# A hybrid decoder layer on one core: fill between chained steps kept on account, the output gate's projection in other loops, states loaded earlier, single-row matmuls in bursts of two tiles

## The chip, the core and the metric

The kernel runs on one core of a Trainium2 chip. Its engines run side by side and wait for each other through semaphores: TensorE (PE for its matmuls, PEld for its weight loads), VectorE (DVE), ScalarE (ACT), GpSimd (POOL) and SyncE (SP), which here issues most DMAs. The metric is device time in microseconds (us); lower is better.

## What is computed

One layer of a decoder serves a prompt of 512 rows and a group of samples, 8 x 4 = 32 rows, with the same weights, all in float32, width 1024. Cut to what matters:

```
h = rms_norm(x, g_mix_pre);  z = h @ w_in
q, k, v, o, gates = mLSTM columns of z (4 heads x 128);  dq, dk, dv = attention columns
h_ml = rms_norm(mlstm(q, k, v, gates, state)) * sigmoid(o)
a = (softmax(dq1 dk1) - lam * softmax(dq2 dk2)) dv        # samples: over cached pages too
x = x + rms_norm(concat(h_ml, rms_norm(a)) @ w_out)
x = x + rms_norm(cross_attention(x, memory))
c = causal_conv3(rms_norm(x) @ w_up);  x = x + rms_norm((silu(c_g) * c_a) @ w_down)
```

The mLSTM of the prompt runs in chunks with a carried matrix state (a chain); that of the samples reads and updates a 128 x 128 state for each of 8 samples and 4 heads. New states, keys, values and conv rows are outputs as well.

## The kernel before

Weights are cast into a high and a low float32r half (`split`, lines 140 to 143), and each product of a k tile is three matmuls. `gemmA` puts token rows out on partitions (blocks 0 to 3 of 128 prompt rows, block 4 with the 32 sample rows); `gemmB` puts weight columns out on partitions, for results that are wanted transposed. Weights pass through staging tiles `wst` (six) into `wslot` tiles (four), in the order of a plan (`Weights`). The 32 sample rows, the "single rows" of the change's title, do not use the split: `sample_mm` (line 359) multiplies them in plain float32 with the staged weights, a pair of k tiles as four matmuls of 32 columns, each to its own 32 partitions of PSUM. In the profile such a matmul is two records, so a pair is x8; in the order it is x4.

The program's text is handed to a scheduler that orders each engine's instructions itself; the text sets priorities and dependences.

Much of the middle is chained work in small steps: the chunks of the prompt's mLSTM (`ml_own`, `ml_state`, `ml_rows`, four steps), the state updates of the samples (`mls_update`, eight, two groups of four samples by four heads), the loop over cached keys (`dk_load`, `dk_turn`, `dk_scores`) and over cached values (`dv_load`, `dv_out`), both with the prompt's attention (`da_soft`, `da_turn`, `da_av`, `da_end`) between their steps. Large matmuls are dealt out between these steps by `Fill`: a queue of generators (`gemmA` for `dk`, `dq`, `dv`, then `gemmB` for the output gate `soT`), each of whose pieces tells its length in us (2.99 for a k tile of all five blocks, 1.36 for two k tiles of `gemmB`); `F.run(amount)` takes pieces until the amount is used up. A last piece that goes beyond the amount is not counted against the next call.

A state update (lines 943 to 959): the states of a group, `Cs`, are loaded (tag `T2`, eight buffers for all small tiles), the queries are multiplied with all four heads' states of a group (`mlsi`, line 949), the update is a matmul `mlus` (line 952), four VectorE steps change `Cs` in place (line 954), and it is written out (line 956); group 1's loads are issued behind group 0's outputs. The gate's sigmoid and the transposition of the mLSTM's result stand in `out_gate`, added to the fill in the loop over cached keys. PSUM has five tiles `mm` and three tiles `at`, the latter for `mlsi`, `mlus`, and the transpositions `tpk` of cached keys.

Of the kernel before, what the change touches and what calls it, by code (L numbers as in the profile page):

```python
# [15 lines left out]
P = 128  # L16
# [6 lines left out]
H = 4  # L23
# [50 lines left out]
def kernel(ctx: ExitStack, tc: tile.TileContext, I, O):  # L74
# [60 lines left out]
    dma = nc.sync.dma_start  # L135
# [191 lines left out]
    allb = [0, 1, 2, 3, 4]  # L327

    class Fill:


        def __init__(self):
            self.q = []

# [3 lines left out]
        def run(self, amount=1e9):  # L338
            while amount > 0 and self.q:
                try:  # L340
                    amount -= next(self.q[0])
                except StopIteration:
                    self.q.pop(0)

    F = Fill()
# [28 lines left out]
    def gemmA(xt, nk, blocks, evac, block_major=False, before=None, mid=None, late=False):  # L374
# [15 lines left out]
        if block_major:  # L390
            slots = [W.get() for _ in range((nk + 1) // 2)]
            for b in blocks:
                if before:
                    before(b)
                ps[b] = mmp()
                for k in range(nk):
                    if k == MIDK and mid:
                        mid()
                    one(b, k, slots[k // 2])
                    if b == blocks[-1] and k % 2 == 1:  # L400
                        W.free()
                evac(b, ps[b])
                yield 5.1
        else:
            for b in blocks:
                ps[b] = mmp()
            behind = []
            for k in range(nk):
                if k % 2 == 0:
                    s = W.get()  # L410
                    if 4 in blocks:
                        behind.append((k, s))
                        if not late:
                            one(4, *behind.pop(0))
                for b in blocks:
                    if b < 4:
                        one(b, k, s)
                if k % 2 == 1:
                    if len(behind) > 1:
                        one(4, *behind.pop(0))  # L420
                    if not late or k > 1:
                        W.free()
                yield sum(0.64 if b < 4 else 0.43 for b in blocks)
            for k, s in behind:
                one(4, k, s)
                W.free()
            for b in blocks:
                evac(b, ps[b])
            yield 0
# [336 lines left out]
    def ev_dv(b, ps):  # L766
# [4 lines left out]
        else:  # L771
# [3 lines left out]
    soT = S([P, H, ROWS], F32, "soT")  # L775
    F.add(gemmA(hT, 8, allb, ev_dk), gemmA(hT, 8, allb, ev_dq), gemmA(hT, 8, allb, ev_dv),
          gemmB(hT, [ev_T(soT, h) for h in range(H)]))

# [39 lines left out]
    def ml_own(b):  # L818
        c0 = b * P
        dms[b] = ml_scores(b)  # L820
        pk = at("mlk")
        for h in range(H):
            tr(pk[:, h * P:(h + 1) * P], kT[:, h, c0:c0 + P], ident)
        wks[b] = T2([P, H, P], "wk")
        VTT(out=wks[b], in0=v2(pk, P), in1=gt4[:, b, 3].unsqueeze(2).broadcast_to([P, H, P]), op=MUL)
        F.run(6)

    def ml_state(b):
# [6 lines left out]
        for hp in range(2):  # L835
# [9 lines left out]
            else:  # L845
                VCP(out=Cn[:, 2 * hp:2 * hp + 2], in_=v2(pu[:, :258], 129))
        F.run(3)

    def ml_rows(b):
# [20 lines left out]
        ml_norm(b, num[:, :, 0:P], num[:, :, P], mlh[b])  # L870
        F.run(3)

# [10 lines left out]


    sm_t = ml_scores(4)
    pk = at("mlks")
# [42 lines left out]
    pi = at("mlsi")  # L929
    csts, vzs = {}, {}  # L930

    def mls_values(i):
# [4 lines left out]
            in1=con("selX")[:, 4 * g:4 * g + 4].unsqueeze(2).broadcast_to([P, 4, P]), op=MUL)  # L937

    def mls_load(g, h):
        csts[g, h] = T2([P, 4, P], "Cs")  # L940
        dma(out=csts[g, h], in_=I["state_ml_C"][0, 4 * g:4 * g + 4, h].rearrange("b d e -> d b e"))

    def mls_update(i):
# [13 lines left out]
        if g == 0:  # L957
            mls_load(1, h)
        F.run(2.5)

    for h in range(H):
        mls_load(0, h)
    run(pipe(2 * H, mls_values, mls_update))
# [251 lines left out]

    W.nslots = 2
    prompt = pipe(4 * H, da_soft, lambda i: None, da_turn, da_av, da_end)
    sall = S([P, NB, 260], F32, "das")
    nm, su = small(NB, "snm"), small(NB, "ssu")
    for t, _ in enumerate(pipe(NB, dk_load, dk_turn, dk_scores)):  # L1220
        if t == 3:
            F.add(out_gate())
        F.run(2.5)
        next(prompt)
        F.run(2.5)
    aw, az = sample_softmax(sall, su, cv, con("selD"), "da")
# [23 lines left out]
    for t, _ in enumerate(pipe(NB, dv_load, lambda b: None, dv_out)):  # L1250
        if t % 2 == 0:
            next(prompt, None)
        F.run(2)
    for h in range(H):
# [364 lines left out]
    for gi, js in enumerate(groups):  # L1619
# [6 lines left out]
        nk = len(js)  # L1626

        def one(b, ps, i, s):
            n = P if js[i] < 21 else 64
            t = act[i // 2][:n, i % 2]  # L1630
            st, en = i == 0, i == nk - 1
            if b == 4:
                if i % 2 == 0:
                    sample_mm(ps, [acs[i], acs[i + 1]], s[1], st, i == nk - 2)
                return
# [34 lines left out]
        if not last:  # L1670
            for n0 in (0, 512):
                ps = {b: mmp() for b in allb}
                for i in range(nk):
                    if i % 2 == 0:
                        s = W.get()
                    for b in sorted(allb, reverse=i % 2 == 0):
                        one(b, ps[b], i, s)
                    if i % 2 == 1 or i == nk - 1:
# [6 lines left out]
        def chunk(b, n0):  # L1685
            while len(wd) < (nk // 2 if n0 == 0 else nk):
                wd.append(W.get())
            ps = mmp()
            for i in range(nk):
                one(b, ps, i, wd[(n0 and nk // 2) + i // 2])  # L1690
# [104 lines left out]
```

## Time and profile before

| what | us |
|---|---|
| median of 3 runs (1000.03 to 1001.18) | 1000.25 |
| the profiled execution's own time | 1001.39 |
| its span, first to last instruction | 999.6 |
| TensorE, sum of matmuls of `sample_mm` (line 366): hidden rows x256, FFN x176 | 20.4, 13.8 |
| `gemmB` (line 452) with `fT`, 1872 matmuls | 235.7 |
| the three matmuls of the down projection (lines 1638 to 1640) | 70.7, 69.5, 69.0 |

Times in the profile are from one execution, whose own time is in the table. A row of the chain of waits gives start, length, and what it was; a row of stages gives each engine's busy time in a stretch; a group gives its busy time, the mean of one in ns, and the idle time of its engine before it.

### The profile page before, as it was taken

What the parts mean: (1) busy time and instruction counts of PE and PEld (TensorE: products, weight loads), DVE (VectorE), ACT (ScalarE), POOL (GpSimd) and SP (SyncE); (2) the same over time, 40 slices, a digit from 0 to 9 for tenths busy, and PEclk for the clock granted to TensorE, in tenths of its full rate; (3) what the DMA queues carried; (4) which work ended last, traced back from release to release, by engine and by line L of the source; (5) the groups of instructions that cost most, each with busy time, mean ns of one, the idle gap of its engine ahead of it and who ended that gap; (6) DMA issues with size and microseconds to landing.
All of it is one profiled execution on the core that took longest, in us unless ns stands there. A gap on an engine that the chain in (4) does not pass through costs nothing.

```text
span 999.6 us, 17060 instructions
## 1 busy us (share of the span) xinstructions
PE 970.7 (97%) x6615; PEld 811.2 (81%) x6615; DVE 599.6 (60%) x1129; ACT 389.3 (39%) x746; POOL 196.1 (20%) x389
## 2 busy tenths in 40 slices
PE   8999999999799999999999999999999999999994
PEld 5899777889555778998767789989987997997983
DVE  5835324643586457643653578827848685775677
ACT  5654313434376447633552444242212222222232
POOL 6610000112332114500000264301101110010115
PEclk9999999999799999999999999999999999999997
DMA  8950234151634167785851673143143214215013
GB/s 278 296 162 14 72 85 130 43 183 55 176 109 136 61 210 233 250 260 166 277 214 43 195 237 107 43 129 91 41 115 87 84 46 127 90 42 145 25 47 110
DMA packets 120401, 130.26 MB, mean 130 GB/s; under 512 B 8423, under 2 KB 85832, under 8 KB 120320
## 3 DMA queue, kind: packets, MB, share of 16 engines
q1 hardware_dynamic: 114136, 125.69, 41.0%
q10 hardware_dynamic: 6184, 3.48, 1.2%
q8 instruction: 52, 0.85, 0.4%
q14 instruction: 29, 0.24, 0.1%
HBM read 112.22 MB, written 16.93 MB: 129 GB/s over the span
## 4 chain that ended last, share of the span: by engine, by line
PE 84%; DMA 5%; DVE 5%; issue 2%; POOL 1%; ACT 1%; SPq 0%; DVEq 0%; POOLq 0%; ACTq 0%
PE mm L452 31%; PE mm L386 6%; PE mm L387 6%; PE mm L388 6%; PE mm L440 5%; PE mm L1638 4%; PE mm L1640 4%; PE mm L1639 4%; PE mm L366 3%; PE sda L1179 2%; PE tpk L1384 2%; PE cpo L1365 1%; PE sca L1335 1%; PE ssc L1394 1%; PE oda L1205 1%
## 5 line engine op out<-in xcount | busy, mean ns | idle before, releaser
L142 ACT CAST wslot<-wst 128x1024 fp32r<-128x1024 f32 (+1 forms) x127 | 131.1, 1036 | 280.2 <-issue 81.5
L452 PE MATMUL mm<-fT,wslot 128*128 128x256 f32 (+1 forms) x1872 | 235.7, 288 | 0.0
L452 PEld LDWEIGHTS mm<-fT,wslot 128*128 128x128 f32 x1872 | 234.7, 188 | 0.7 <-issue 0.4
L143 DVE TENSOR_TENSOR wslot<-wst,wslot 128x1024 fp32r<-128x1024 f32 (+1 forms) x127 | 155.0, 1223 | 107.0 <-ACT wslot L142 106.9
L1638 PE MATMUL mm<-wslot,act 128*128 128x512 f32 (+1 forms) x176 | 70.7, 409 | 0.0
L1639 PE MATMUL mm<-wslot,act 128*128 128x512 f32 (+1 forms) x176 | 69.5, 395 | 0.0
L1640 PE MATMUL mm<-wslot,act 128*128 128x512 f32 (+1 forms) x176 | 69.0, 397 | 0.0
L1545 POOL COPY cvo<-u 128x2 f32<-128x2 f32 x43 | 16.2, 377 | 222.9 <-DVE u L1543 222.9
L386 PE MATMUL mm<-wslot,hT 128*128 128x512 f32 x128 | 51.9, 408 | 0.0
L452 PE MATMUL mm<-hT,wslot 128*128 128x288 f32 (+1 forms) x384 | 51.4, 290 | 0.0
L387 PE MATMUL mm<-wslot,hT 128*128 128x512 f32 x128 | 51.2, 400 | 0.0
L388 PE MATMUL mm<-wslot,hT 128*128 128x512 f32 x128 | 50.7, 397 | 0.0
L452 PEld LDWEIGHTS mm<-hT,wslot 128*128 128x128 f32 x384 | 48.9, 188 | 0.9 <-issue 0.8
L1638 PEld LDWEIGHTS mm<-wslot,act 128*128 128x128 f32 (+1 forms) x176 | 33.1, 189 | 17.7 <-issue 8.6
L1540 DVE TENSOR_TENSOR u<-mm,rsb 128x256 f32<-128x256 f32 x43 | 18.1, 423 | 43.5 <-PE mm L452 43.4
L1640 PEld LDWEIGHTS mm<-wslot,act 128*128 128x128 f32 (+1 forms) x176 | 33.0, 188 | 7.5
L1639 PEld LDWEIGHTS mm<-wslot,act 128*128 128x128 f32 (+1 forms) x176 | 33.1, 188 | 6.5
L1557 ACT ACTIVATE c<-c 128x560 f32<-128x560 f32 x21 | 14.1, 672 | 56.8 <-DVE c L1551 56.7
L1551 DVE SCALAR_TENSOR_TENSOR c<-u,cvT,c 128x560 f32<-128x560 f32 x43 | 34.3, 798 | 0.8
L1550 DVE SCALAR_TENSOR_TENSOR c<-u,cvT,c 128x560 f32<-128x560 f32 x43 | 34.1, 793 | 0.1
L1651 DVE TENSOR_TENSOR yp<-mm,yp 128x512 f32<-128x512 f32 x40 | 27.3, 688 | 9.5 <-PE mm L1640 9.4
L386 PEld LDWEIGHTS mm<-wslot,hT 128*128 128x128 f32 x128 | 24.0, 188 | 10.3 <-issue 5.8
(458 smaller groups left out, 1879.5 us busy)
## 6 DMA issues: line engine op xcount, KB each, us to landing
wst<-in_w_up_dram SPq DMA_DIRECT2D x42, 512.0 KB
wst<-in_w_in_dram SPq DMA_DIRECT2D x28, 512.0 KB
wst<-in_w_down_dram SPq DMA_DIRECT2D x20, 512.0 KB
wst<-in_cache_mem_k_dram SPq DMA_DIRECT2D x16, 512.0 KB
vt<-in_cache_mem_v_dram SPq DMA_DIRECT2D x8, 1024.0 KB
wst<-in_w_mk_dram SPq DMA_DIRECT2D x8, 512.0 KB
xb<-in_x_prompt_dram SPq DMA_DIRECT2D x8, 512.0 KB
wst<-in_cache_dk_dram SPq DMA_DIRECT2D x16, 256.0 KB
```

The lines of the kernel that those rows point to most:

```text
L142: nc.scalar.copy(out=hi, in_=src)
L143: (eng or nc.vector).tensor_tensor(out=lo, in0=src, in1=f32(hi), op=SUB)
L386: mm(ps[b], lhsT=xt.hi(k, c0, c0 + n), rhs=s[:, 0, kk, :], start=(k == 0), stop=False)
L387: mm(ps[b], lhsT=xt.hi(k, c0, c0 + n), rhs=s[:, 1, kk, :], start=False, stop=False)
L388: mm(ps[b], lhsT=xt.lo(k, c0, c0 + n), rhs=s[:, 0, kk, :], start=False, stop=(k == nk - 1))
L440: mm(ps, lhsT=s[:, l, k, :], rhs=x(k, c0, c1), start=(k == 0 and j == 0), stop=(k == 7 and j == 2))
L452: mm(ps[i], lhsT=s[:, l, k, :], rhs=x(k, c0, c1), start=(k == 0 and j == 0), stop=(k == 7 and j == 2))
L1550: STT(out=c, in0=u[:, 1:EXT - 1], scalar=w[1], in1=c, op0=MUL, op1=ADD)
L1551: STT(out=c, in0=u[:, 0:EXT - 2], scalar=w[0], in1=c, op0=MUL, op1=ADD)
L1638: mm(ps, lhsT=t[:, 0, c0:c0 + P], rhs=s[:n, 0, i % 2, :], start=st, stop=False)
L1639: mm(ps, lhsT=t[:, 0, c0:c0 + P], rhs=s[:n, 1, i % 2, :], start=False, stop=False)
L1640: mm(ps, lhsT=t[:, 1, c0:c0 + P], rhs=s[:n, 0, i % 2, :], start=False, stop=en)
```

## The change

It changes five things. `Fill` keeps an account: what a call takes too much is owed, and paid by the next calls; the amounts are changed with it. The gate's projection leaves the first queue, which is emptied ahead of the loop over cached keys, and is queued there, with 0.9 (twice a step) and 1 us a step. The loads of group 0's states stand ahead of the samples' scores. `gemmA` and the down projection collect the sample rows of two k-tile pairs, and put them out as one burst. The diff, cut to what matters:

```diff
@@ -330,17 +330,21 @@
 
 
         def __init__(self):
-            self.q = []
+            self.q, self.due = [], 0
 
         def add(self, *gens):
             self.q.extend(gens)
 
         def run(self, amount=1e9):
-            while amount > 0 and self.q:
+
+            self.due += amount
+            while self.due > 0 and self.q:
                 try:
-                    amount -= next(self.q[0])
+                    self.due -= next(self.q[0])
                 except StopIteration:
                     self.q.pop(0)
+            if not self.q:
+                self.due = 0
 
     F = Fill()
 
@@ -410,19 +414,22 @@
                     s = W.get()
                     if 4 in blocks:
                         behind.append((k, s))
-                        if not late:
-                            one(4, *behind.pop(0))
+                        if k % 4 == 2 and not late:
+                            while behind:
+                                one(4, *behind.pop(0))
                 for b in blocks:
                     if b < 4:
                         one(b, k, s)
                 if k % 2 == 1:
-                    if len(behind) > 1:
-                        one(4, *behind.pop(0))
+                    if k == 5:
+                        while len(behind) > 1:
+                            one(4, *behind.pop(0))
                     if not late or k > 1:
                         W.free()
                 yield sum(0.64 if b < 4 else 0.43 for b in blocks)
             for k, s in behind:
                 one(4, k, s)
+            if behind:
                 W.free()
             for b in blocks:
                 evac(b, ps[b])
@@ -773,8 +780,7 @@
             dma(out=O["s_dv"][0].rearrange("b t h d -> (b t) (h d)"), in_=dvS)
 
     soT = S([P, H, ROWS], F32, "soT")
-    F.add(gemmA(hT, 8, allb, ev_dk), gemmA(hT, 8, allb, ev_dq), gemmA(hT, 8, allb, ev_dv),
-          gemmB(hT, [ev_T(soT, h) for h in range(H)]))
+    F.add(gemmA(hT, 8, allb, ev_dk), gemmA(hT, 8, allb, ev_dq), gemmA(hT, 8, allb, ev_dv))
 
 
     def ml_scores(b):
@@ -823,7 +829,7 @@
             tr(pk[:, h * P:(h + 1) * P], kT[:, h, c0:c0 + P], ident)
         wks[b] = T2([P, H, P], "wk")
         VTT(out=wks[b], in0=v2(pk, P), in1=gt4[:, b, 3].unsqueeze(2).broadcast_to([P, H, P]), op=MUL)
-        F.run(6)
+        F.run(5)
 
     def ml_state(b):
         if b % 2 == 0:
@@ -844,7 +850,7 @@
                         op0=MUL, op1=ADD)
             else:
                 VCP(out=Cn[:, 2 * hp:2 * hp + 2], in_=v2(pu[:, :258], 129))
-        F.run(3)
+        F.run(2.5)
 
     def ml_rows(b):
         c0 = b * P
@@ -868,7 +874,7 @@
             else:
                 VCP(out=nv, in_=v2(pn[:, :258], 129))
         ml_norm(b, num[:, :, 0:P], num[:, :, P], mlh[b])
-        F.run(3)
+        F.run(2.5)
 
     run(pipe(4, ml_own, ml_state, ml_rows))
     C = Cs[3]
@@ -882,6 +888,14 @@
     dma(out=O["p_ml_n"][0, 0], in_=nrow)
 
 
+    csts, vzs = {}, {}
+
+    def mls_load(g, h):
+        csts[g, h] = T2([P, 4, P], "Cs")
+        dma(out=csts[g, h], in_=I["state_ml_C"][0, 4 * g:4 * g + 4, h].rearrange("b d e -> d b e"))
+
+    for h in range(H):
+        mls_load(0, h)
     sm_t = ml_scores(4)
     pk = at("mlks")
     for h in range(H):
@@ -927,18 +941,12 @@
     dma(out=O["s_ml_n"][0].rearrange("b h d -> (b h) d"), in_=nrow1)
 
     pi = at("mlsi")
-    csts, vzs = {}, {}
-
     def mls_values(i):
 
         g, h = i // H, i % H
         vzs[i] = T2([P, 4, P], "vz", F32R)
         GTT(out=vzs[i], in0=f32(vS[:, h, :]).unsqueeze(1).broadcast_to([P, 4, P]),
             in1=con("selX")[:, 4 * g:4 * g + 4].unsqueeze(2).broadcast_to([P, 4, P]), op=MUL)
-
-    def mls_load(g, h):
-        csts[g, h] = T2([P, 4, P], "Cs")
-        dma(out=csts[g, h], in_=I["state_ml_C"][0, 4 * g:4 * g + 4, h].rearrange("b d e -> d b e"))
 
     def mls_update(i):
         g, h = i // H, i % H
@@ -956,10 +964,8 @@
         dma(out=O["s_ml_C"][0, 4 * g:4 * g + 4, h].rearrange("b d e -> d b e"), in_=cs_t)
         if g == 0:
             mls_load(1, h)
-        F.run(2.5)
-
-    for h in range(H):
-        mls_load(0, h)
+        F.run(3.2)
+
     run(pipe(2 * H, mls_values, mls_update))
     pn = at("mlsn")
     for h in range(H):
@@ -1214,15 +1220,17 @@
     STT(out=cv, in0=con("cB"), scalar=nlam, in1=con("cA"), op0=MUL, op1=ADD)
 
     W.nslots = 2
+    F.run()
+    F.add(gemmB(hT, [ev_T(soT, h) for h in range(H)]))
     prompt = pipe(4 * H, da_soft, lambda i: None, da_turn, da_av, da_end)
     sall = S([P, NB, 260], F32, "das")
     nm, su = small(NB, "snm"), small(NB, "ssu")
     for t, _ in enumerate(pipe(NB, dk_load, dk_turn, dk_scores)):
         if t == 3:
             F.add(out_gate())
-        F.run(2.5)
+        F.run(0.9)
         next(prompt)
-        F.run(2.5)
+        F.run(0.9)
     aw, az = sample_softmax(sall, su, cv, con("selD"), "da")
     F.run(4)
     pz = Z("pz")[:, :NS]
@@ -1250,7 +1258,7 @@
     for t, _ in enumerate(pipe(NB, dv_load, lambda b: None, dv_out)):
         if t % 2 == 0:
             next(prompt, None)
-        F.run(2)
+        F.run(1)
     for h in range(H):
         mm(ops[NS * h:NS * h + NS, :P], lhsT=anew[:, h].rearrange("p b t -> p (b t)"), rhs=dvS[:, h * P:(h + 1) * P],
            start=False, stop=True)
@@ -1625,13 +1633,19 @@
         act, acs = acts[gi], acss[gi]
         nk = len(js)
 
+        behind = []
+
         def one(b, ps, i, s):
             n = P if js[i] < 21 else 64
             t = act[i // 2][:n, i % 2]
             st, en = i == 0, i == nk - 1
             if b == 4:
-                if i % 2 == 0:
-                    sample_mm(ps, [acs[i], acs[i + 1]], s[1], st, i == nk - 2)
+
+                behind.append((i, s))
+                if i % 4 == 2 or i == nk - 2:
+                    for j, t in behind:
+                        sample_mm(ps, [acs[j], acs[j + 1]], t[1], j == 0, j == nk - 2)
+                    behind.clear()
                 return
             s = s[0]
             c0 = b * P
@@ -1674,7 +1688,8 @@
                     if i % 2 == 0:
                         s = W.get()
                     for b in sorted(allb, reverse=i % 2 == 0):
-                        one(b, ps[b], i, s)
+                        if b < 4 or i % 2 == 0:
+                            one(b, ps[b], i, s)
                     if i % 2 == 1 or i == nk - 1:
                         W.free()
                 for b in allb:
@@ -1686,7 +1701,7 @@
             while len(wd) < (nk // 2 if n0 == 0 else nk):
                 wd.append(W.get())
             ps = mmp()
-            for i in range(nk):
+            for i in range(0, nk, 2 if b == 4 else 1):
                 one(b, ps, i, wd[(n0 and nk // 2) + i // 2])
             add_y(b, ps, n0)
 
```

What the scheduler makes of it is seen in the order of instructions. TensorE at the down projection of the first FFN group (`act` the gated rows, `acs` their sample rows), before:

```order
L452 MATMUL mm<-fT_6087,wslot 128x288
L366 MATMUL mm<-wst,acs 32x256 x4
L1638 MATMUL mm<-wslot,act 128x512
L1639 MATMUL mm<-wslot,act 128x512
L1640 MATMUL mm<-wslot,act 128x512
```

and in the changed kernel, some thirty matmuls of the prompt later (its lines 370 and 1652 to 1654 are lines 366 and 1638 to 1640 of before):

```order
L1652 MATMUL mm<-wslot,act 128x512
L1653 MATMUL mm<-wslot,act 128x512
L1654 MATMUL mm<-wslot,act 128x512
L370 MATMUL mm<-wst,acs 32x256 x8
L1654 MATMUL mm<-wslot,act 128x512
```

The burst at the start of the group is gone; it stands with the second one, further down, and the two are one.

TensorE at the end of the state updates, before (`sda` and its mask `cb` belong to the prompt's attention, `mlsn` to the samples' result, `tpk` to the first cached keys):

```order
L1179 MATMUL sda<-dkT,dqT 128x128
L1180 LDWEIGHTS cb
L1180 MATMUL sda<-cb 128x128
L952 MATMUL mlus<-vz,kS 128x512
L949 MATMUL mlsi<-Cs,qzm 32x128 x14
L952 MATMUL mlus<-vz,kS 128x512 x4
L966 MATMUL mlsn<-tb,mlD 32x128 x4
L1158 MATMUL tpk<-cpk,wst 128x128 x16
```

and in the changed kernel (lines 957, 960, 972 and 1164 are 949, 952, 966 and 1158 of before; 459 is 452, the gate's projection):

```order
L960 MATMUL mlus<-vz,kS 128x512
L459 MATMUL mm<-hT_255,wslot 128x288
L459 MATMUL mm<-hT_255,wslot 128x256
L459 MATMUL mm<-hT_255,wslot 128x288
L459 MATMUL mm<-hT_256,wslot 128x256
L459 MATMUL mm<-hT_256,wslot 128x288
L957 MATMUL mlsi<-Cs,qzm 32x128 x13
L459 MATMUL mm<-hT_255,wslot 128x256
L459 MATMUL mm<-hT_255,wslot 128x288
L960 MATMUL mlus<-vz,kS 128x512 x3
L972 MATMUL mlsn<-tb,mlD 32x128 x4
L1164 MATMUL tpk<-cpk,wst 128x128 x16
```

Matmuls of the gate's first head now stand between the later updates; the last three `mlus` still follow each other.

SP's queue around the state loads, before:

```order
L882 DMA out_dram<-nrow 4x128
L900 DMA nrow_2292<-in_state_ml_n_dram 32x128
L941 DMA Cs<-in_state_ml_C_dram 128x4x128
L927 DMA out_dram<-nrow_2321 32x128
L941 DMA Cs<-in_state_ml_C_dram 128x4x128 x5
L956 DMA out_dram<-Cs 128x4x128 x2
L941 DMA Cs<-in_state_ml_C_dram 128x4x128 x2
L956 DMA out_dram<-Cs 128x4x128 x5
```

and in the changed kernel (895 and 964 are 941 and 956 of before; 777 the outputs of `dv`, 246 the gate's weights, 1051 the gathers of cached keys):

```order
L895 DMA Cs<-in_state_ml_C_dram 128x4x128
L941 DMA out_dram<-nrow_1971 32x128
L895 DMA Cs<-in_state_ml_C_dram 128x4x128
L964 DMA out_dram<-Cs 128x4x128 x2
L777 DMA out_dram<-dvN 128x512 x3
L895 DMA Cs<-in_state_ml_C_dram 128x4x128
L246 DMA wst<-in_w_in_dram 128x8x128 x2
L1051 ISA
L1051 DMA wst<-in_cache_dk_dram 128x512
```

Before, all eight loads of states stood close together, with twelve gathers of keys ahead of them. Now the fifth to seventh are shown here, and the eighth follows behind seven gathers.

## The prediction

> **What bounds the kernel now.** I read the page's busy shares first, then its slices.
>
> ```profile
> span 999.6 us, 17060 instructions
> PE 970.7 (97%) x6615; PEld 811.2 (81%) x6615; DVE 599.6 (60%) x1129; ACT 389.3 (39%) x746; POOL 196.1 (20%) x389
> PEclk9999999999799999999999999999999999999997
> ```
>
> TensorE is named busy for 970.7 of 999.6 us, so what shortens its work, or fills a hole in it, shortens the kernel, and no other engine is near. The clock row has two dips: one behind the end, and one in the eleventh slice, near 260 us. So next I asked for the stages around that dip (columns: length, then busy time of PE, PEld, DVE, ACT, POOL with counts, granted clock, DMA share, GB/s).
>
> ```profile
> 255.20:268.00 12.80, 7.33 (x48) 3.68 (x48) 8.44 (x33) 2.23 (x10) 5.14 (x5) 0.65 0.46 137
> 268.00:273.00 5.00, 5.00 (x26) 3.64 (x27) 2.65 (x9) 1.62 (x5) 0.95 (x3) 0.52 0.98 294
> 273.00:307.00 34.00, 32.57 (x229) 19.59 (x233) 27.82 (x75) 24.76 (x80) 11.34 (x13) 1.00 0.36 110
> 307.00:332.00 25.00, 24.40 (x233) 13.94 (x226) 17.52 (x34) 17.19 (x48) 4.57 (x6) 1.00 0.52 174
> ```
>
> The first row is the tail of the state updates of the samples: TensorE idle for 12.80 - 7.33 = 5.47 us. Row two is the first cached keys, at half clock. Rows three and four are the loop over cached keys and the one over cached values: idle 1.43 + 0.60 = 2.03 us. The chain of waits says why the first hole is there (start, length, what).
>
> ```profile
> 250.90 0.41 PE mlsi L949 x7
> 251.31 1.63 DVE Cs L954 x6
> ...
> 253.18 4.60 DMA out_dram<-Cs
> ...
> 257.80 2.97 DMA Cs<-in_state_ml_C_dram
> ...
> 260.81 1.92 PE mlsi L949 x26
> ...
> 264.01 1.62 DVE Cs L954 x6
> ...
> 267.86 3.65 PE tpk L1158 x16
> 271.51 1.03 PE ssc L1164 x8
> ...
> 274.08 0.88 PE tpk L1158 x8
> 274.96 0.57 PE ssc L1164 x8
> ```
>
> A state is updated, written out (4.60 us), only then is its buffer free for the next load (2.97 us), and `mlsi` waits for that load. No projection is left by then to fill the time: the gate projection has ended at 253 us.
>
> **Term 1, bursts of single rows.** A pair of k tiles costs four matmuls of 32 columns, recorded as eight. The chain around a single and a double burst:
>
> ```profile
> 649.45 0.24 PE mm L1640
> 649.68 0.57 PE mm L366 x8
> 650.25 0.43 PE mm L1638
> ...
> 658.57 0.24 PE mm L1640
> 658.80 1.00 PE mm L366 x16
> 659.80 0.43 PE mm L1638
> ```
>
> The matmul behind a burst holds the chain 0.43 us, against 0.24 for its like ahead of it, 0.19 more. A single burst so costs 0.57 + 0.19 = 0.76, a double one 1.00 + 0.19 = 1.19, and two singles made one save 2 x 0.76 - 1.19 = 0.33 us. Counted in the order on TensorE, 41 runs become 30: 11 x 0.33 = 3.6 us, of which four are in the conv FFN, one for each group of four tiles. Their other half brings nothing, since there the order of before already had x8. Over all 32-column work, changes between narrow and wide matmuls fall from 203 to 173, that is by 15 round trips; 11 are the bursts, the other four (mainly `mlsi`, which stood as 1, 1, 1, 13 and is now 16) would bring 1.3 us at the same price. Ends -3.6 and -5.0; I take **-5.0**, since a round trip is the same thing there.
>
> **Term 2, the state updates.** What is lost in the first two stages is the idle 5.47 us and the half clock. For the latter: `tpk` took 3.65 us for 16, against 2 x 0.88 at full clock, 1.9 more; `ssc` 1.03 against 0.57, 0.5 more; 26 records of `mlsi` 1.92 against 26 x 0.41 / 7 = 1.52, 0.4 more. Together 2.8, and the loss is 8.3 us. With the fill on account the dv projection reaches into the updates, and the gate projection's first head stands between the later ones, so the first wait (a load behind an output) has work beside it. Two pieces stay. One is the last four updates: they read the last four loaded states, and TensorE has little to put beside them.
>
> ```profile
> 263.49 4.23 DVE L954 SCALAR_TENSOR_TENSOR Cs<-Cs,dec,mlus 128x128 f32<-128x128 f32 x16 [3.81 <-PE mlus L952]
> PE mlsi L949 <- DMA Cs<-in_state_ml_C_dram: 3.5, 2, 1.9
> 269.83 2.56 SPq L1045 DMA_DIRECT2D wst<-in_cache_dk_dram  x4
> wst<-in_cache_dk_dram SPq DMA_DIRECT2D x16, 256.0 KB
> ```
>
> VectorE needs 4.23 us for those 16 steps, and the next `tpk` waits for a PSUM tile that they hold; beside them the new order has 13 `mlsi` (26 records, 1.5 us), two gate matmuls, three `mlus` and four `mlsn`, some 2.2 us in all: 2.0 us stay. The other is the eighth load: on SP's queue it now stands behind two weight tiles (512 KB each) and seven key gathers of 256 KB (0.64 us apiece on the queue, by 2.56 for four). These 2.8 MB need 9.6 us at the 294 GB/s of stage two. They can start when the dv projection's sample bursts let go of the staging tiles, and from there TensorE has, by the order, some 11 us until the `mlsi` that need the eighth. So nothing to 4 us; I take 1.0, near the even race. Ends: -8.3 (all goes) and +0.5 (the first piece stays whole at a half clock, and 4 us more wait for the load). Taken: -8.3 + 3.0 = **-5.3**.
>
> **Term 3, the loops over cached tokens.** Three heads of the gate projection, 144 matmuls, come here; they cost nothing in sum, having left the stretch before.
>
> ```profile
> 671.11 35.94 PE mm L452 x288
> ```
>
> At 35.94 / 288 = 0.125 us that is 18 us of work for steps that now take 34.0 / 10 = 3.4 us and hold 1.43 us of plain idle. VectorE was busy 27.82 of 34, and loses here the gate's multiplications, so TensorE becomes the longer by far, and the idle in both loops goes: -2.0. More may go, since "busy" covers waits as well (weight loads are busy 19.59 of 34 only): down to -5.0. Against it, ScalarE:
>
> ```profile
> 253.59 0.66 ACT L987 ACTIVATE soT<-soT 128x544 f32<-128x544 f32 x1
> 254.26 1.28 ACT L1183 ACT_TABLE_LOAD   x1
> 255.55 0.37 ACT L1183 ACTIVATE pda<-sda,nm 128x128 f32<-128x128 f32 x1
> L617 ACT COPY soT<-mm 128x256 f32<-128x256 f32 (+1 forms) x8 | 2.7, 388 | 16.3 <-PE mm L452 16.3
> ```
>
> The four sigmoids of the gate now stand among the softmax exponentials, so eight table loads are in the loops where the four of before were ahead of them: 8 x 1.28 + 4 x 0.66 + 2.7 = 15.6 us more on an engine that was busy 24.76 of 34. In 34 + 18 = 52 us that is 40.4, covered, unless the exponential behind a load is the one that TensorE waits for; also the gate's two accumulators leave three of five `psm` tiles to the loop. Bounds are nothing and the 17.2 us of rival (c); I take +0.8, 0.2 for each sigmoid, since the cover is there. Taken: **-1.2**. The Trainium skill ("ScalarE: Activation LUTs", What ACT_TABLE_LOAD costs) says that each switch also drains for about 1.38 us; by its price the loops would carry 51 of 52 us on ScalarE, an estimate, and the gain here would be gone. This trace does not agree: the exponential starts at 255.55, as the load ends.
>
> **Nothing for the rest.** The stretch with the chained steps, before:
>
> ```profile
> 97.00:216.00 119.00, 119.00 (x667) 89.68 (x660) 50.44 (x121) 36.44 (x68) 9.31 (x15) 1.00 0.33 91
> ```
>
> TensorE is never idle in it, and VectorE, the busiest of the chain's engines, is so 42% of the time. A step gets about 10 us of fill instead of some 21, since an overshoot is now paid back. Ten us still lie between a step's matmuls and the next step's, so I cost it at nothing; if VectorE's chain showed through at the end of each of four steps, at half a microsecond each, 2 us. A burst for two pairs holds the staging tiles two k tiles longer; the loads behind it start later, at a DMA share of 0.33, and are cost at nothing too, ends 0 and +1.
>
> **The sum.** -5.0 - 5.3 - 1.2 = -11.5 on the profiled execution's own 1001.39 us (span 999.6): 989.9. That execution was 1.14 above the median of 1000.25, so **988.8 us**. Own range of this case 985 to 993.
>
> **The rivals.**
> (a) *The cover is wider than I say*: all of term 2 goes, and term 3 reaches -5.0. For it: weight loads idle for 14 of 34 us. Against: the 16 steps on VectorE. 1000.25 - 5.0 - 8.3 - 5.0 = 982.0. Chance 0.15.
> (b) *The wait moves to the eighth load*: behind the gathers it comes 4 us late, not 1, and the tail falls to half clock again (2.8). 988.8 + 3.0 + 2.8 = 994.6. For it: SP issues in order, and the dip of before came although the longest of those waits was 1.9 us. Chance 0.18. The Trainium skill ("TensorE: Matmul & The Clock Gate", Part 1) has the clock fall after an idle window of about 3.4 us; by that the tail, whose waits are each near 1 us, would stay at full clock, and (b) would be 991.8. The rows speak against so simple a rule: clock down within 255 to 260 us with no idle of 3.4 us.
> (c) *Slower: the exponentials wait behind the sigmoids.* At each of four places TensorE stands for two loads, a sigmoid, and the restart of one softmax step: 2 x 1.28 + 0.66 = 3.2, plus the restart, taken as three times the 0.37 us of an exponential, 1.1; 4 x 4.3 = 17.2 in place of 0.8: 1005.2. It decides from 3.6 us a place on (13.5 us more than forecast). Against it: two steps lie between an exponential and its transposition, some 10 us with the fill. Chance 0.08.
> (d) *It doesn't do what it says*: the fill is spent elsewhere, terms 2 and 3 are zero, and only the eleven bursts count: 996.6. Chance 0.07.
>
> **How the numbers follow.** Forecast 0.52. The likeliest is 988.8. The range 981 to 997 takes in (a), (b) and (d) and leaves out (c) and the tails, less than 2 in 10. About 0.2%, 2 us, is what a measurement can tell from no change: faster means below 998.2, with the forecast, (a), (b) and most of (d): 0.92, less 0.05 for the tail of the forecast and of (d) that reach into no change: 0.87. Same: 0.05. Slower, above 1002.3, is (c): 0.08.
>
> **What would show it.** Double bursts (x16) in the FFN where x8 stood, the following matmul still at 0.43. In the state updates: no chain piece of an output followed by a state load; a wait of `mlsi` under 1.5 us, then some 2 us ahead of `tpk`; the clock row without its middle dip. In the key loop, gate matmuls between `ssc` and `oda`, and idle of TensorE below 1 us with more than 44 us for the ten steps. It is wrong if `sda` waits for `pda` at the sigmoids, if `mlsi` waits longer than before for a state, or if the dip is still there.

## The result, and the profile after

The changed kernel takes 1012.11 us (median of 5 runs, 1010.07 to 1013.53), the kernel before 1001.18 in the same session: ratio 1.0097, 95% interval 1.0079 to 1.0116. It is slower by about 1%; the prediction was 988.8, with a range that ended at 997. The page after, its span, busy shares and the row of the granted clock:

```profile
span 1008.3 us, 17081 instructions
...
PE 973.2 (97%) x6615; PEld 816.6 (81%) x6615; DVE 601.2 (60%) x1129; ACT 393.3 (39%) x750; POOL 196.5 (19%) x389
...
PEclk9999999989989799999999999999999999999998
```

TensorE is named busy for 2.5 us more than before although it does the same matmuls with fewer changes between narrow and wide ones, and the one dip in the middle has become three. One stretch holds the difference: from the first matmuls of `v` (97.9 us) to the last one of the projection with `w_out`. Ahead of it TensorE's idle time differs by 0.3 us; behind it the new one gains 1.7 us, 1.5 of them in the conv FFN. The row of that stretch, before and after (length, busy time of PE, PEld, DVE, ACT, POOL, clock, DMA share, GB/s):

```profile
97.90:384.90 287.00, 279.50 (x1792) 207.14 (x1789) 145.88 (x356) 124.32 (x290) 53.23 (x77) 0.98 0.38 115
```

```profile
97.90:395.30 297.40, 283.87 (x1801) 211.94 (x1800) 147.17 (x356) 128.80 (x294) 53.00 (x76) 0.95 0.35 111
```

It is 10.4 us longer. Idle of TensorE goes from 7.5 to 13.5 us (length less busy), and the clock from 0.98 to 0.95: the trace has it at half from 218.28 for 6.83 us, from 286.55 for 6.83 and from 330.92 for 13.65, together twice the 13.65 us of before. That costs at most 6.8 us more, an estimate that takes TensorE at half speed for all of it. With the 6.0 us of idle it is 2.4 us more than the 10.4, about what the bursts bring by the run of them alone below.

By stage (state updates, loop over keys, its end, loop over values up to the first projection matmul):

```profile
206.80:246.30 39.50, 34.03 (x264) 25.88 (x261) 29.57 (x93) 11.56 (x27) 9.66 (x11) 0.91 0.61 198
246.30:297.80 51.50, 48.88 (x351) 36.02 (x344) 24.60 (x74) 33.21 (x89) 9.53 (x17) 0.93 0.33 106
297.80:312.30 14.50, 14.03 (x91) 8.97 (x90) 6.21 (x16) 9.74 (x28) 2.36 (x3) 1.00 0.00 0
312.30:339.80 27.50, 22.53 (x197) 12.04 (x196) 17.64 (x31) 15.38 (x36) 9.10 (x10) 0.84 0.46 159
```

Three stages have idle and a low clock: 5.5 us idle in the updates, 2.6 in the loop over keys, 5.0 in the loop over values, where before TensorE missed 0.6. The idle of the updates is as long as before (5.5 us); that of the loop over values is new. The chain of waits says what each is. In the updates:

```profile
213.39 1.01 PE mlsi L957 x32
214.40 0.44 PE mlus L960
...
215.13 0.87 DVE Cs L962 x3
...
216.02 2.83 DMA out_dram<-Cs
...
218.94 0.23 DVE rp L739
```

A state is written out, and only then does `rp` start, the temporary of the rotation of `dq`: it is a `T2` tile, as the states are. So not only a load, but the fill itself now waits for an output. In the loop over keys:

```profile
282.08 0.66 ACT soT L993
...
284.02 1.28 ACT L1189
285.30 0.01 issue
285.31 0.57 ACT pda L1189 x2
285.89 0.04 issue
285.93 1.07 PE sda L1185 x2
```

A sigmoid, a table load (the row of ScalarE without a tile), the exponential, and then the scores `sda` that wait for it: rival (c), at this place and at 267 us, in the waits of TensorE (total, times, longest):

```profile
PE sda L1185 <- ACT pda L1189: 2.2, 2, 1.5
```

In the loop over values, where most is lost, the waits of ScalarE, and SP's queue:

```profile
ACT wslot L142 <- DMA wst<-in_w_out_dram: 4.7, 1, 4.7
```

```profile
257.61 59.26 SPq L1051 DMA_DIRECT2D wst<-in_cache_dv_dram  x14
316.98 6.67 SPq L227 DMA_DIRECT2D wst<-in_w_out_dram  x6
```

The six staging tiles are full of cached values from early on, and the transfers stand still: 0 GB/s in the row of 297.80 to 312.30. The weights of the projection can be loaded only when the first matmuls with values (`ops`) let tiles go. ScalarE's next instruction is the cast of such a tile, so that it stands for 4.7 us, and behind it the softmax of the prompt's attention (`pda` its exponentials, `aT` their transposes, `dao` its copied outputs):

```profile
PE oda L1211 <- ACT dao L1213: 1.5, 1, 1.5
PE tpa L1201 <- DVE pda L1193: 1.3, 1, 1.3
PE sda L1185 <- ACT pda L1189: 1.2, 1, 1.2
PE oda L1211 <- ACT aT L1203: 1.1, 1, 1.1
```

Four waits of TensorE, about 5 us, and the half clock that follows them.

### The profile page after: what moved, and what is told of

Read it like the earlier page. It is cut to its first block, busy times and chain, and to the rows that moved or that the text cites. A ratio compares the mean times of both kernels' runs of the same rounds, so it can differ in the third digit from the quotient of the medians.

```text
span 1008.3 us, 17081 instructions
## 1 busy us (share of the span) xinstructions
PE 973.2 (97%) x6615; PEld 816.6 (81%) x6615; DVE 601.2 (60%) x1129; ACT 393.3 (39%) x750; POOL 196.5 (19%) x389
## 4 chain that ended last, share of the span: by engine, by line
PE 79%; DMA 6%; DVE 6%; issue 3%; ACT 3%; POOL 2%; SPq 1%; DVEq 0%; POOLq 0%; ACTq 0%
PE mm L459 30%; PE mm L390 6%; PE mm L391 5%; PE mm L392 5%; PE mm L447 5%; PE mm L1652 4%; PE mm L1654 4%; PE mm L1653 4%; PE mm L370 3%; DMA xb<-x_d 2%; PE tpk L1392 1%; PE sda L1185 1%; DMA wst<-in_w_mk_dram 1%; PE cpo L1373 1%; PE sca L1343 1%
## 5 line engine op out<-in xcount | busy, mean ns | idle before, releaser
L459 PE MATMUL mm<-hT,wslot 128*128 128x256 f32 (+1 forms) x384 | 55.5, 298 | 0.0
L459 PEld LDWEIGHTS mm<-hT,wslot 128*128 128x128 f32 x384 | 51.1, 194 | 2.8 <-issue 1.9
L1665 DVE TENSOR_TENSOR yp<-mm,yp 128x512 f32<-128x512 f32 x40 | 27.3, 689 | 13.7 <-PE mm L1654 13.6
L1185 PE MATMUL sda<-dkT,dqT 64*128 64x128 f32 (+3 forms) x64 | 28.5, 527 | 3.5 <-ACT pda L1189 3.4
```

The source lines that it names most:

```text
L459: mm(ps[i], lhsT=s[:, l, k, :], rhs=x(k, c0, c1), start=(k == 0 and j == 0), stop=(k == 7 and j == 2))
L1185: mm(sv[c], lhsT=dqT[rr, h, c0:c0 + P], rhs=dkT[rr, h, 0:nk], start=True, stop=False)
```

## The experiments

Ratios are against the kernel before, run on the same chip beside them; us in brackets behind a ratio are medians. The medians of before differ a little from session to session (1000.45 to 1001.19), so where two other kernels are compared, it is by their distances from the before of their own session; the changed kernel is 10.9 us above its own. A ratio is not the quotient of two medians: by the ratios such distances come out up to some 2 us different (18.8 in place of 20.0, 3.3 in place of 5.4), so none of them is surer than that.

**The bursts alone** (the kernel before with the changes to `gemmA` and to the down projection, measured twice):

```diff
-                        if not late:
-                            one(4, *behind.pop(0))
+                        if k % 4 == 2 and not late:
+                            while behind:
+                                one(4, *behind.pop(0))
```

> The kernel before with the bursts of two k-tile pairs alone (gemmA and the down projection); fill without account, amounts, gate and state loads as before. If a round trip between narrow and wide matmuls costs 0.33 us wherever it stands, this is 3.6 to 5.0 us faster than before, about 1.3 of it in the conv FFN. Rival: the bursts hold staging tiles longer and delay the weights behind them, then it is within 1 us of before, with new waits of mm for wslot.

> The bursts alone once more, to size them: the first seven runs gave 2.4 us, their profiled execution 4.7 us less than that of before. If a round trip costs what the prediction took: ratio 0.995; if half of that: 0.9975.

Measured: 0.9975, interval 0.9964 to 0.9986 (998.04), and again 0.9964, 0.9951 to 0.9977 (997.62): 2.4 and 3.3 us faster. The eleven bursts were priced at 3.6, which lies at the edge of the first interval (1.4 to 3.6 us) and inside the second (2.3 to 4.9). The further 1.4 us of term 1, for four other round trips, are not tested by it: `mlsi` still stands there as before, one, one, one and thirteen matmuls. The delay of weights isn't seen: TensorE waits for a `wslot` once, 0.3 us, in either run. The price itself is as in the rows of before, here from the FFN of the changed kernel:

```profile
663.03 1.00 PE mm L370 x16
664.03 0.43 PE mm L1654
```

**The states not ahead** (the changed kernel):

```diff
-    for h in range(H):
-        mls_load(0, h)
     sm_t = ml_scores(4)
...
+    for h in range(H):
+        mls_load(0, h)
     run(pipe(2 * H, mls_values, mls_update))
```

> The changed kernel with the loads of the first group's states back where they stood before. Theory: the four states loaded ahead hold half of the eight T2 buffers, so that the temporaries of the dq projection's rotation wait for a state's output; without them the stall at 215 to 220 us and the half clock behind it (together some 7 us) shrink, 1012 becomes 1006 to 1009. Rival: the stall is that of the update itself (output, then load, then mlsi), which then comes back as it was in the kernel before: within 2 us of the changed kernel, with mlsi waiting for a load of Cs.

Measured: 1.0137, 1.0122 to 1.0153 (1014.34), 3 us slower than the changed kernel. The first theory falls: the states ahead help, though little. That is a microsecond more than the rival's 2, but `mlsi` waits for a load as it said:

```profile
PE mlsi L955 <- DMA Cs<-in_state_ml_C_dram: 3.5, 1, 3.5
```

**The gate's projection ahead of the loops:**

```diff
-    F.run()
     F.add(gemmB(hT, [ev_T(soT, h) for h in range(H)]))
+    F.run()
```

> The changed kernel with the gate's projection added to the queue ahead of the call that empties it, so that no matmul of it stands in the loops. Theory: both the waits for the exponentials in the key loop (some 4 us, and 3.4 us of half clock) and the crowded value loop (some 3 us, and up to 7 us of half clock) come from the gate's work and its sigmoids in the loops; 1012 becomes 997 to 1001, with two half-clock stretches less. Rival: the loss is the updates' alone, and the loops lose as much without the fill as with it: 1009 to 1013.

Measured: 0.9909, 0.9894 to 0.9924 (991.36). That is 6 us below the range of the theory. Two exchanged lines are worth 20 us, and the rest of the change is a gain of 9. The loop over values is again as it was before, without a low clock:

```profile
296.80:322.10 25.30, 24.70 (x240) 14.04 (x240) 17.85 (x35) 17.20 (x48) 4.55 (x6) 1.00 0.51 172
```

**No table loads in the loops** (the changed kernel):

```diff
-            ACT(out=soT[:, h], in_=soT[:, h], func=AF.Sigmoid)
+            ACT(out=soT[:, h], in_=soT[:, h], func=AF.Exp, scale=-1.0)
+            nc.gpsimd.tensor_scalar(out=soT[:, h], in0=soT[:, h], scalar1=1.0, scalar2=1.0, op0=ADD, op1=MUL)
+            nc.vector.reciprocal(out=soT[:, h], in_=soT[:, h])
```

> The changed kernel with the gate's sigmoid made of an exponential, an addition on GpSimd and a reciprocal on VectorE, so that no table load stands between the softmax exponentials; the fill stays where it is. Theory (sigmoids' table loads make the exponentials late): the waits of sda for pda at 267 and 284 to 288 us and the half clock behind the second go, 1012 becomes 1004 to 1007. Rival: the value loop's late weights and gathers set its end anyway, so what is won in the key loop is waited for there: 1009 to 1012.

Measured: 1.0065, 1.0041 to 1.0089 (1008.1), between the two. It is 3.3 us faster than the changed kernel: rival (c) is real, but a sixth of the 20 us. The idle of the stretch falls from 13.5 to 10.8 us, and its clock falls with it, from 0.95 to 0.94, so that in this execution the gain is given back (at 1010.23 us it is 2.1 above the median of this kernel, so the row says little about its size):

```profile
97.90:395.20 297.30, 286.47 (x1800) 213.41 (x1792) 160.23 (x360) 119.04 (x286) 57.57 (x81) 0.94 0.35 111
```

**Half of the gate in the loops:**

```diff
+    F.add(gemmB(hT, [ev_T(soT, h) for h in range(2)]))
     F.run()
-    F.add(gemmB(hT, [ev_T(soT, h) for h in range(H)]))
+    F.add(gemmB(hT, [ev_T(soT, h) for h in range(2, H)]))
```

> The changed kernel with two of the gate's four heads added ahead of the call that empties the queue, and two behind it: half of the gate's matmuls stand in the loops, but they and the sigmoids end well ahead of the loop over values. If each head in the loops costs the same, this lies half way between 991.4 (none) and 1012.1 (all): 1000 to 1003. If what costs is that the gate's end and its sigmoids run into the start of the loop over values (and push the loads of w_out behind it), most of the loss is gone: 993 to 997, with no half clock between 320 and 345 us.

Measured: 0.9924, 0.9903 to 0.9945 (991.86), the same as with none, and a microsecond below the expected range. The loss is not a fixed amount for each head in the loops.

**The gate thinner, over both loops:**

```diff
-        F.run(0.9)
+        F.run(0.45)
         next(prompt)
-        F.run(0.9)
+        F.run(0.45)
...
-        F.run(1)
+        F.run(1.5)
```

> The changed kernel with half the gate's fill in the loop over keys (0.45 in place of 0.9 us, twice a step) and 1.5 in place of 1 us a step in the loop over values, so that the projection really spreads over both loops. If the idle beside the late loads of w_out is for want of matmuls, the gate's fill it, and the time falls to 1001 to 1006. Rival: the gate's weights and its sigmoids, now in the loop over values, push w_out's loads and the exponentials further back: 1012 to 1020.

Measured: 1.011, 1.0093 to 1.0127 (1011.17), as the changed kernel, a microsecond below the rival's range. Its 17 transpositions come later still, at 319.2 to 331.6 us. More matmuls in the loop over values do not help by themselves.

**The gate faster:**

```diff
-        F.run(0.9)
+        F.run(1.8)
         next(prompt)
-        F.run(0.9)
+        F.run(1.8)
```

> The changed kernel with twice the gate's fill in the loop over keys (1.8 in place of 0.9 us, twice a step), so that the same matmuls stand in that loop, but in its first half, and the sigmoids and the transpositions behind them end before the loop over values. If what costs is the gate's end at the start of the loop over values, this is as fast as with two heads: 991 to 996. If three heads in the loops cost what they are, wherever they stand: 1006 to 1012.

Measured: 0.9917, 0.9891 to 0.9942 (992.7). The same matmuls in the same loop, only earlier in it, and 19 us are gone. This number alone separates the changed kernel from a gain. The stretch, and the loop over values, now:

```profile
97.90:379.30 281.40, 274.65 (x1802) 206.87 (x1801) 147.51 (x356) 128.48 (x294) 53.56 (x77) 0.98 0.36 117
...
300.10:326.10 26.00, 24.99 (x241) 13.97 (x240) 17.37 (x33) 16.71 (x47) 4.42 (x6) 1.00 0.49 168
```

The idle is 6.8 us, half of that of the changed kernel. SP's queue has the loads of `w_out` spread over 12.20 us where it had 6.67:

```profile
308.63 12.20 SPq L227 DMA_DIRECT2D wst<-in_w_out_dram  x6
```

**Late transpositions alone** (all matmuls of the gate ahead, as in `e3_gate_first`; the edit moves the text of `out_gate`, sigmoids and transpositions both):

```diff
-        if t == 3:
-            F.add(out_gate())
...
+    F.add(out_gate())
     F.run(4)
     pz = Z("pz")[:, :NS]
```

> The kernel with all of the gate's matmuls ahead of the loops (e3_gate_first), but with its sigmoids and the 17 transpositions behind them put between the loop over keys and the loop over values, where the changed kernel has them. If these alone, ahead of the first matmul with cached values, push the loads of w_out back and leave TensorE without cover there: 998 to 1003, with a half clock between 320 and 345 us. If it takes the gate's matmuls too: 990 to 994.

Measured: 1.0001, 0.9986 to 1.0016 (1001.93): 10 us more than with the same matmuls and `out_gate` early. The scheduler did not follow the text in all: the four sigmoids start at 241.84 to 261.26 us, about as in `e3_gate_first` (240.56 to 259.97), and only the 17 transpositions, with the multiplications and casts behind them, are late (297.7 to 302.7 us in place of 264.9 to 272.2). So about half of the loss needs neither a matmul of the gate in the loops nor a late sigmoid. Its end of the loops, first the row up to the projection, then the chain:

```profile
295.70:330.30 34.60, 31.65 (x256) 17.70 (x255) 22.85 (x42) 20.24 (x55) 10.74 (x11) 0.82 0.38 126
```

```profile
305.05 1.05 PE sda L1185 x2
306.26 2.32 PE ops L1254 x80
...
310.13 6.77 DMA wst<-in_w_out_dram
316.96 0.37 ACT dao L1213
317.37 0.65 PE tpa L1201 x4
318.03 1.98 PE sda L1185 x2
```

Eighty records of `ops` stand in one row. In the kernel before three steps of the prompt's attention stand between them; here, and in the changed kernel, one more of these has been done ahead of the first `ops`, beside the transpositions (36 records of `oda` in place of 30), so less is left beside the loads. TensorE idles 1.6 us ahead of 318.0 us, and from there the clock is at half for 17.1 us, with TensorE named busy for 16.3 of them. `e3_gate_first` has no such stretch in its loop over values or in the projection, so of the 10 us at most some 8 are half clock, an estimate. First starts and last ends of the matmuls in five traces:

| kernel | first `ops` starts | last `ops` of cached values ends | first projection matmul | first `ops` to projection |
|---|---|---|---|---|
| before | 311.6 | 326.4 | 331.6 | 20.0 |
| `e3_gate_first` | 302.1 | 316.8 | 322.1 | 20.0 |
| `e10_fast` | 305.8 | 320.4 | 326.1 | 20.3 |
| `e11_late_gate` | 306.2 | 314.6 | 330.3 | 24.1 |
| changed | 313.5 | 323.2 | 339.8 | 26.3 |

**Casts of `w_out` on GpSimd** (the changed kernel, and then `e11_late_gate`):

```diff
+        if share == "pool":
+            nc.gpsimd.tensor_copy(out=sv[:, 0], in_=st)
+            nc.gpsimd.tensor_tensor(out=sv[:, 1], in0=st, in1=f32(sv[:, 0]), op=SUB)
+            return
...
-        slotsA(w_out, n0)
+        slotsA(w_out, n0, share="pool" if n0 == 0 else False)
```

> The changed kernel with the first four tiles of w_out cast and split on GpSimd, where ScalarE casts them in the changed kernel. If the 4.7 us in which ScalarE waits at 319 to 324 us for a weight tile hold the softmax's steps behind it, these go: 1003 to 1008, without the half clock from 331 us on. If the projection waits for the weights' landing anyway: 1009 to 1014.

Measured: 1.0064, 1.0042 to 1.0085 (1006.72), 5.4 us faster than the changed kernel, as expected, and the loop over values has no low clock any more:

```profile
298.00:331.20 33.20, 32.72 (x286) 19.40 (x285) 19.15 (x39) 20.80 (x59) 15.90 (x15) 1.00 0.40 131
331.20:390.10 58.90, 55.80 (x299) 42.33 (x298) 25.43 (x40) 25.16 (x51) 20.74 (x25) 1.00 0.34 111
```

The projection behind it takes 58.9 us and idles 3.1, where the kernel before took 53.3 us (331.6 to 384.9) without idle time: a part of the wait has only moved there.

> The kernel with the gate's matmuls ahead and its sigmoids and transpositions late (e11_late_gate, 1001.9), with the first four tiles of w_out cast on GpSimd. If what the late transpositions cost is ScalarE's wait for those tiles, with the softmax behind it: 993 to 997. If it is that TensorE has nothing left beside the loads, whoever casts them: 1000 to 1003.

Measured: 0.9977, 0.9961 to 0.9993 (998.69), between the two expectations: 3 of the 10 us are won back. In its trace the clock is not at half in the loop over values, and the projection starts at 321.1 us in place of 330.3, but TensorE then idles 3.9 us of the next 48.9. That the weights come late to the projection costs something whoever casts them; how the rest divides is not settled by this run.

**Both remedies at once** (`e4_exp` and `e14_pool_cast`):

> The changed kernel with both remedies that helped it alone, the exponential in place of the sigmoid (4.0 us) and the casts of w_out on GpSimd (5.4 us). If they mend two separate waits: 1001 to 1004. If both mend the same wait, in the loop over values: 1005 to 1008. If they together are the whole loss against the faster fill: 992 to 995.

Measured: 1.005, 1.003 to 1.0071 (1006.02). That is in the range for one and the same wait (5.8 us together, 3.3 and 5.4 alone), but by the ratios it is 4.7 against 3.2 and 3.3, each some 2 us unsure, so that they do not add up is not shown. Together they stay 14 us behind the plain increase of an amount.

**Temporaries out of `T2`** (on `e3_gate_first`), and the exponential with it:

```diff
-        t = T2([P, 2, 8, 16], "rp")[:n]
+        t = N("rp", 256).rearrange("p (a b c) -> p a b c", a=2, b=8)[:n]
```

> The kernel with the gate's projection ahead of the loops (e3_gate_first), and the temporaries of the rotation of dk and dq out of the T2 buffers, in another pool. Theory: at 215 to 221 us the rotation's temporary waits for a buffer that a state holds until it is written out; without it some 1 to 2 us of wait and the half clock behind it (2.8 us) go: 986 to 989. Rival: mlsi waits there for a state's load in any case: 990 to 993.

Measured: 0.9888, 0.9872 to 0.9905 (989.59). The wait goes, as the rows of 213 to 222 us show, first without and then with this edit:

```profile
213.00:222.00 9.00, 5.30 (x47) 3.63 (x38) 6.85 (x31) 1.74 (x4) 1.74 (x2) 0.78 0.31 89
```

```profile
213.00:222.00 9.00, 8.27 (x65) 5.39 (x64) 4.97 (x23) 2.05 (x4) 2.09 (x2) 0.62 0.48 129
```

Idle falls from 3.7 to 0.7 us, but the half clock stays, and the interval overlaps that of `e3_gate_first`; the time lies between the two expectations, and a gain is possible and not shown.

> The gate's projection ahead of the loops, the rotation's temporaries out of the T2 buffers (e6_rp), and the sigmoid made of an exponential, an addition and a reciprocal (as in e4_exp): 986 to 990 if the table loads still hold TensorE up where the gate stands at the start of the loop over keys, 989 to 991 if they are covered there.

Measured: 0.99, 0.9878 to 0.9922 (991.6), just above both expected ranges: no further gain is seen, as if the table loads were covered there.

**No account:**

```diff
     W.nslots = 2
+    F.run()
     prompt = pipe(4 * H, da_soft, lambda i: None, da_turn, da_av, da_end)
```

The kernel before with the bursts, the states ahead and this line.

> The kernel before with the bursts, the states loaded ahead, and the queue emptied ahead of the loop over keys, but without the account and its amounts, and with the gate's projection in the first queue. Theory: the account is what leaves fill for the state updates, so their idle and half clock (8.3 us) stay: 996 to 999. Rival: the states loaded ahead suffice: 990 to 993, as with the account.

Measured: 0.9953, 0.9937 to 0.9969 (996.52). Against `e3_gate_first`, 0.9909, the account and its amounts bring 4 to 5 us, as the theory had it.

## Why the prediction was wrong

**Where it failed: term 3.** The step was "they cost nothing in sum, having left the stretch before", and "TensorE becomes the longer by far, and the idle in both loops goes". It took -1.2 us; the place of the gate costs about +20 (10.9 us above the kernel before against 9.1 below it with the gate ahead of the loops). It counted cover inside each loop, 18 us of matmuls for ten steps, and never asked when the last piece ends and what stands behind it. At 0.9 us twice a step the gate lasts beyond the end of the loop over keys (its last matmuls end at 302.2 us); its last sigmoid (304.37) and its 17 transpositions (303.0 to 311.6) then stand ahead of the first matmul with values, and on that matmul hang the staging tiles, on these the loads of `w_out`, on these ScalarE's next cast. Shown: with the same matmuls ending by the middle of the loop (277 us) the time is 992.7; with late transpositions alone it is 1001.9. The other half of the 20 us, from late matmuls and late sigmoids, is shown as a sum only. Against the faster fill, the stretch from 97.9 us is 16.0 us longer in the changed kernel: 6.7 of it idle (13.5 less 6.8), and at most 8.5, an estimate, from 27.3 us at half clock in place of 10.2. The chain from the staging tiles to the cast is read from the trace; of its last link, the cast, the run with casts on GpSimd shows 3 to 5 us.

**Rival (c)** had the sign, a chance of 0.08 and 1005.2. Its mechanism shows at two places of the four, and the run without table loads gives it 3.3 us of the 17.2. The measured time lies 7 us above its 1005.2, mostly for another reason; the sign was partly luck.

**Term 1** was of the right kind: -5.0, of which the eleven bursts at 0.33 us make 3.6, and the runs of the bursts alone have -2.4 and -3.3. In the conv FFN its four bursts, 1.3 us, are there (1.5 by the traces). The price was extended to four round trips of other matmuls, and no run shows these by themselves.

**Term 2**, -5.3, can be read with term 1 from the kernel with the gate ahead of the loops: predicted -10.3 together, measured -9.1. So the sum came out near where the gate was out of the way, with the account (4 to 5 us) and the states ahead (3 us, measured in the changed kernel). That is partly luck, since the pieces were not those named. The eighth load was no matter; the sixth was: it left SP only at 215.26, since its `T2` buffer was that of a row still being written out, and `mlsi` waited for it. SP's waits, and TensorE's:

```profile
SPq L895 <- DMA out_dram<-nrow: 1.1, 1, 1.1
```

```profile
PE mlsi L957 <- DMA Cs<-in_state_ml_C_dram: 1.6, 1, 1.6
```

The tail ahead of `tpk` was taken at 2.0 us, and the idle from 240.0 to 247.5 us is 7.50 less 5.33, 2.2.

```profile
240.00:247.50 7.50, 5.33 (x56) 3.66 (x56) 6.48 (x23) 1.36 (x6) 3.27 (x4) 1.00 0.91 301
```

That eight `T2` tiles serve states and the fill's temporaries alike was in the text on the kernel, and not in the prediction.

**Nothing for the rest** was right: TensorE has no idle time from 97.9 to 206.8 us in the changed kernel.

**What would show it:** of its three signs against, two came, `sda` waiting for `pda` and the dip, and the third, a longer wait of `mlsi`, did not (1.6 us against 1.9).

## What to carry to other kernels

When work is spread as fill through a loop, ask first when its last piece ends and what is queued behind that, and only then whether each step is covered: here 1.8 in place of 0.9 decided between 8 us won and 11 us lost. Look with care at a loop whose buffers also carry the next stage's weights: where it started late here, little was left to hide their load. Where one edit of several fails, take it out alone before doubting the others: the remaining ones were worth 9 us.

## What the hardware showed beside

The granted clock moves in steps of 3.41 us: every stretch at half clock ahead of the last matmuls, in all these runs, is a multiple of it (3.41 to 17.07 us). Behind one step with 1.48 us of idle it was halved for two, while behind one with 1.22 us (242.17 to 245.58) it stayed up; no run sets a threshold. Five such steps of the changed kernel (the clock is the third number from the end):

```profile
279.72:283.13 3.41, 3.41 (x26) 2.41 (x28) 1.89 (x4) 3.38 (x9) 0.29 (x1) 1.00 0.18 34
283.13:286.55 3.42, 1.94 (x16) 0.99 (x8) 1.11 (x4) 3.39 (x9) 1.69 (x2) 1.00 0.32 119
286.55:289.96 3.41, 3.41 (x13) 0.91 (x12) 1.78 (x4) 1.74 (x7) 0.00 (x0) 0.50 0.00 0
289.96:293.37 3.41, 3.41 (x19) 3.40 (x16) 2.24 (x9) 0.93 (x4) 0.00 (x0) 0.50 0.01 2
293.37:296.78 3.41, 3.41 (x24) 2.72 (x23) 0.20 (x1) 0.74 (x2) 1.76 (x1) 1.00 0.00 0
```

So a wait of 1.5 us was followed by a loss of up to 3.4 us of work, an estimate: two steps at half clock. And records that fill a step do not keep the clock up: in `e6_rp` it falls behind a stretch that is named busy throughout, for most of it by narrow matmuls (`mldn`, `mlg`, `mlsi`):

```profile
211.44:214.85 3.41, 3.41 (x52) 2.80 (x54) 1.45 (x9) 0.00 (x0) 0.00 (x0) 1.00 0.27 77
214.85:218.27 3.42, 2.80 (x25) 1.35 (x14) 1.60 (x7) 0.00 (x0) 1.04 (x1) 0.50 0.28 77
```

The Trainium skill ("TensorE: Matmul & The Clock Gate", Part 1) has a free-running window of 3413 ns, which agrees, and lets the clock fall after one idle window or more; here it fell after a window that was 57% busy by the records, and after a full one.
